# Splitting weight blocks behind the evacuation, and attention halves six items ahead

## The chip, the cores and the metric

The kernel runs on one core of one Trainium2 chip. The metric is the device time of one execution in microseconds (us); the median of several runs is compared. TensorE (PE) multiplies matrices; its loads of stationary operands are shown apart as PEld. VectorE (DVE) and ScalarE (ACT) evacuate results and prepare operands, GpSimd (POOL) starts accumulating DMAs and does a few small operations, and SyncE (SP) starts most DMAs.

## The reference

One decoder layer over 512 tokens of width 1024, in float32. A combined input projection gives q, k and v for three attention branches and three gate vectors; the branch outputs are projected, gated, summed and projected once more; two layer norms, a squared-ReLU MLP and a gated per-layer embedding follow.

```python
proj = x @ w_in
(da_q, da_k, da_v, sb_q, sb_k, sb_v, dl_q, dl_k, dl_v, gates) = jnp.split(proj, _split_points(), axis=-1)
o_da = diff_attention(...)            # 4 heads, two softmax maps per head
o_sb = stick_breaking_attention(...)  # 8 heads
o_dl = dilated_attention(...)         # 3 groups x 4 heads
g = jax.nn.sigmoid(gates).reshape(B, S, N_BRANCHES, D)
merged = (g[:, :, 0] * (o_da @ w_branch_da) + g[:, :, 1] * (o_sb @ w_branch_sb)
          + g[:, :, 2] * (o_dl @ w_branch_dil))
m = merged @ w_out
x = layer_norm(DEEPNORM_ALPHA * x + m, ln1_g, ln1_b)
c = jnp.square(jax.nn.relu(x @ w_up)) @ w_down
ple = jax.nn.sigmoid(x @ w_ple_gate) * (p @ w_ple)
x = layer_norm(DEEPNORM_ALPHA * x + c + ple, ln2_g, ln2_b)
```

## The kernel before

**Halves.** Each float32 operand of a large product is split into a high half in the rounded matmul type (fp32r) and a low half, the remainder. A product of two such operands takes three matmuls: high by high, high by low, low by high. A weight block is 128 x 1024 numbers. It is loaded by SP into one of five `raw` buffers (`RAW = 5`, line 223, function `fill`), cast by ACT into `wh` (line 255), and DVE subtracts to make `wl` (line 258); both lie in rings of seven (`RING = 7`). `split_next` does this for the next block in a fixed list (`chunks`). Some blocks are sums of two loaded ones; DVE adds them in place first (line 244). Other sums are made in DRAM by accumulating DMAs on POOL (line 190), after copies that SP starts (line 186).

**Items.** The work of PE is a list of 312 items, each with the blocks it needs, the blocks it releases (`it["c"]`), a function `mm` that issues its matmuls into a PSUM bank, and a function `ev` that evacuates the bank. Items 0 to 58 are the input projections: a T item makes 128 columns of q or k (24 products of 0.39 us each, one block), and a group of four V items makes 512 columns of v with four blocks, released by the last. Items 59 to 72, 73 to 86 and 95 to 108 are the three gates, each done with seven instead of eight block products (`seven`), two items for each product `p`, r = 0 and 1, with two blocks. Items 87 to 94, 109 to 116 and 117 to 124 are the three branch projections (`branch`, twelve products per item); they need the halves `oTh`, `oTl` of the attention outputs, which `halves(k)` makes on ACT or DVE (cast, lines 93 and 95) and DVE (line 574). Items 125 to 132 are the output projection, 133 to 154 the embedding gate and the embedding itself, 155 to 302 the MLP as alternating groups of up items (line 881 on) and down items (line 968 on), and from 303 the last block row, done plainly. In three up and three down groups of the MLP ("mixed") and in the second and third gate some of the blocks are sums made by DVE. Attention itself runs beside the items: generators for the heads are advanced by `step()`, between items and in the middle of a T item.

**The loop.** For item n the program runs the functions hooked to n (`at`, among them `halves` and the sigmoids), splits blocks that the item can't do without, issues the evacuation of item n-1, calls `pump`, starts other work that is due by number (the load of `pT` at item `first_branch + 3` = 112), issues the matmuls of n, adds the blocks that it releases to `freed`, and calls `pump` again. `pump(limit, most)` splits up to `most` blocks while fewer than `freed + 7` are split, and lets `fill` issue the loads that the raw buffers allow. From item 10 on both calls have `most` = 2.

**Order.** Each engine takes its own instructions strictly in the order of its queue. That order is made when the kernel is built: a planner in the framework goes through the program with its own estimates of durations, takes what it holds to be ready, and settles ties by the order in which the program wrote the instructions. It also gives out the 46 slots of 128 x 512 numbers in SBUF (`slot`) in which q, k, v, evacuated results, attention outputs and halves lie. So an edit of the program's order moves priorities, not places.

## Time and profile before

| what | value |
|---|---|
| median of 3 runs | 1076.69 us (1075.1 to 1078.05) |
| the profiled execution | 1074.75 us |
| its span, first to last instruction | 1073.1 us |
| PE busy | 1047.6 us, 98% |
| PEld busy | 898.1 us, 84% |
| DVE busy | 775.9 us, 72% |
| ACT busy | 557.2 us, 52% |
| POOL busy | 87.2 us, 8% |
| granted TensorE clock, mean | 0.994 |
| DMA | 209.12 MB, mean 195 GB/s |

The profile is of one execution, taken by the hardware profiler. A row of the timeline gives start, duration, engine, line of the program, operation, output and inputs, and in brackets how long the engine had been idle and what released it. Matmuls overlap: a product is shown with 0.39 us and one starts every 0.23 us. In the groups, "x245" is the count, followed by the busy time, the mean duration in ns, and the idle time just before with its releaser. The granted clock (PEclk) is the share of full speed that the chip allowed TensorE. The chain is the work that ended last, followed back from the end through what released each step.

### The profile page before, as it was taken

What the parts mean: (1) busy time and instruction counts of PE and PEld (TensorE: products, weight loads), DVE (VectorE), ACT (ScalarE), POOL (GpSimd) and SP (SyncE); (2) the same over time, 40 slices, a digit from 0 to 9 for tenths busy, and PEclk for the clock granted to TensorE, in tenths of its full rate; (3) what the DMA queues carried; (4) which work ended last, traced back from release to release, by engine and by line L of the source; (5) the groups of instructions that cost most, each with busy time, mean ns of one, the idle gap of its engine ahead of it and who ended that gap; (6) DMA issues with size and microseconds to landing.
All of it is one profiled execution on the core that took longest, in us unless ns stands there. A gap on an engine that the chain in (4) does not pass through costs nothing.

```text
span 1073.1 us, 14737 instructions
## 1 busy us (share of the span) xinstructions
PE 1047.6 (98%) x5503; PEld 898.1 (84%) x5503; DVE 775.9 (72%) x1328; ACT 557.2 (52%) x908; POOL 87.2 (8%) x107
## 2 busy tenths in 40 slices
PE   9999999999999899999999899999999999999996
PEld 6877788999888688888888788888989989989985
DVE  6888576545453567987757765898788788788786
ACT  6566444435242445786626322365756556557551
POOL 0000101000010100101101100100001011110000
PEclk9999999999999999999999999999999999999999
DMA  7454564428888664375967975347867978976712
GB/s 273 158 216 177 197 255 100 97 75 238 236 256 208 172 207 138 94 240 138 298 176 228 323 250 163 116 151 247 250 201 204 287 185 215 275 181 196 234 59 79
DMA packets 64140, 209.12 MB, mean 195 GB/s; under 512 B 7501, under 2 KB 10461, under 8 KB 62916
## 3 DMA queue, kind: packets, MB, share of 16 engines
q1 hardware_dynamic: 43108, 167.38, 43.2%
q0 software_dynamic: 20384, 39.88, 21.5%
q8 instruction: 43, 0.70, 0.2%
q10 hardware_dynamic: 576, 0.92, 0.2%
q14 instruction: 29, 0.24, 0.1%
HBM read 206.03 MB, written 77.62 MB: 264 GB/s over the span
## 4 chain that ended last, share of the span: by engine, by line
PE 95%; DVE 3%; ACT 1%; issue 1%; DMA 0%; POOL 0%; DVEq 0%; SPq 0%; ACTq 0%
PE mm L84 6%; PE mm L85 6%; PE mm L86 6%; PE mm L881 5%; PE mm L882 5%; PE mm L883 5%; PE mm L363 3%; PE mm L365 3%; PE mm L364 3%; PE at L451 3%; PE at L453 3%; PE at L454 3%; PE mm L968 2%; PE mm L969 2%; PE mm L970 2%; PE mm L600 2%
## 5 line engine op out<-in xcount | busy, mean ns | idle before, releaser
L255 ACT CAST wh<-raw 128x1024 fp32r<-128x1024 f32 x245 | 254.9, 1049 | 250.9 <-PE mm L85 44.6
L258 DVE TENSOR_TENSOR wl<-raw,wh 128x1024 fp32r<-128x1024 f32 x245 | 296.5, 1223 | 112.5 <-ACT wh L255 103.9
L84 PE MATMUL mm<-xhT,wh 128*128 128x512 f32 x304 | 121.6, 400 | 1.3 <-DVE da_qb L105 1.1
L86 PE MATMUL mm<-xhT,wl 128*128 128x512 f32 x304 | 119.6, 394 | 0.0
L85 PE MATMUL mm<-xlT,wh 128*128 128x512 f32 x304 | 119.6, 393 | 0.0
L881 PE MATMUL mm<-XH,wh 128*128 128x256 f32 x256 | 72.8, 285 | 5.1 <-DVE xn L975 2.5
L882 PE MATMUL mm<-XL,wh 128*128 128x256 f32 x256 | 72.5, 283 | 0.0
L883 PE MATMUL mm<-XH,wl 128*128 128x256 f32 x256 | 72.5, 283 | 0.0
L84 PEld LDWEIGHTS mm<-xhT,wh 128*128 128x128 f32 x304 | 57.5, 189 | 15.1 <-issue 3.9
L86 PEld LDWEIGHTS mm<-xhT,wl 128*128 128x128 f32 x304 | 57.4, 189 | 12.4 <-DVE wl L258 0.4
L85 PEld LDWEIGHTS mm<-xlT,wh 128*128 128x128 f32 x304 | 57.5, 189 | 10.8
L363 PE MATMUL mm<-wh,xhT 128*128 128x512 f32 x160 | 64.1, 402 | 0.0
L365 PE MATMUL mm<-wh,xlT 128*128 128x512 f32 x160 | 63.3, 396 | 0.0
L364 PE MATMUL mm<-wl,xhT 128*128 128x512 f32 x160 | 63.2, 395 | 0.0
L881 PEld LDWEIGHTS mm<-XH,wh 128*128 128x128 f32 x256 | 49.1, 192 | 6.5 <-issue 4.6
L882 PE MATMUL mm<-xs,wh 128*128 128x256 f32 x192 | 54.4, 283 | 0.0
L883 PE MATMUL mm<-xs,wl 128*128 128x256 f32 x192 | 54.4, 283 | 0.0
L881 PE MATMUL mm<-xs,wh 128*128 128x256 f32 x192 | 54.4, 283 | 0.0
L882 PEld LDWEIGHTS mm<-XL,wh 128*128 128x128 f32 x256 | 49.1, 192 | 0.2
L883 PEld LDWEIGHTS mm<-XH,wl 128*128 128x128 f32 x256 | 49.1, 192 | 0.0
L190 POOL DMA_DIRECT2D total<-total x26 | 23.9, 936 | 279.9 <-ACT wh L255 264.5
L365 PEld LDWEIGHTS mm<-wh,xlT 128*128 128x128 f32 x160 | 38.0, 238 | 3.8
(421 smaller groups left out, 2563.2 us busy)
## 6 DMA issues: line engine op xcount, KB each, us to landing
raw<-total SPq DMA_DIRECT2D x72, 512.0 KB, 5.8
raw<-in_wt_dram SPq DMA_DIRECT2D x38, 512.0 KB, 7.0
total<-in_wu_dram SPq DMA_DIRECT2D x26, 512.0 KB, 8.4
total<-total POOLq DMA_DIRECT2D x26, 512.0 KB, 9.3
raw<-in_wd_dram SPq DMA_DIRECT2D x25, 512.0 KB, 5.5
raw<-in_wu_dram SPq DMA_DIRECT2D x24, 512.0 KB, 4.9
total<-in_wd_dram SPq DMA_DIRECT2D x22, 512.0 KB, 7.3
raw<-in_wv_dram SPq DMA_DIRECT2D x20, 512.0 KB, 4.0
```

The source lines that it names most:

```text
L84: nc.tensor.matmul(ps, wh, xh, start=start, stop=False, skip_group_check=True)
L85: nc.tensor.matmul(ps, wh, xl, start=False, stop=False, skip_group_check=True)
L86: nc.tensor.matmul(ps, wl, xh, start=False, stop=stop, skip_group_check=True)
L255: i = nc.vector.tensor_copy(h, raw) if c.get("dve") else nc.scalar.copy(h, raw)
L258: i = nc.vector.tensor_sub(lo, raw, h.bitcast(F32))
L363: nc.tensor.matmul(ps, x1, c["h"][:, s], start=k == 0, stop=False)
L364: nc.tensor.matmul(ps, x1, c["l"][:, s], start=False, stop=False)
L365: nc.tensor.matmul(ps, x2, c["h"][:, s], start=False, stop=k == 7)
L451: nc.tensor.matmul(ps, h, c["h"][:, s], start=k == 0 and begins, stop=False, skip_group_check=True)
L881: nc.tensor.matmul(o, c["h"][:, s], h, start=first, stop=False, skip_group_check=True)
L882: nc.tensor.matmul(o, c["h"][:, s], lo, start=False, stop=False, skip_group_check=True)
L883: nc.tensor.matmul(o, c["l"][:, s], h, start=False, stop=last, skip_group_check=True)
```

## The change

Four edits. In `branch`, `halves(k)` is hooked to item `b0 - 6 + k` and not `b0 - 4 + k`, `b0` being the branch's first item. In the mixed groups of the MLP, block 3 is split ahead of block 4, and block 3 is released by the item that uses it last, not together with blocks 4 and 7. The `pump` behind the evacuation splits one block, and two only where `st["split"] - freed`, the blocks split and not yet released, is at most 3. The `pump` behind an item's matmuls splits nothing from item 10 on (it did not before item 10 either) and only lets `fill` issue loads.

```diff
@@ -575,7 +575,7 @@
                 oTs[4 * i + k] = (h, lo)
 
             for k in range(4):
-                hook(b0 - 4 + k, lambda k=k: halves(k))
+                hook(b0 - 6 + k, lambda k=k: halves(k))
 
@@ -838,8 +838,8 @@
             def mixed_chunks(w, first):
                 raw = {q: load(w[q], 1024) for q in (*first, 5, 3, 7)}
                 c = {p: chunk_of(raw[{6: 5, 4: 5}.get(p, p)], {6: raw[3], 4: raw[2]}.get(p))
-                     for p in (*first, 5, 6, 4, 3, 7)}
-                return c, {6: [], 5: [c[5], c[6]], 7: [], 3: [], 4: [c[4], c[3], c[7]]}
+                     for p in (*first, 5, 6, 3, 4, 7)}
+                return c, {6: [], 5: [c[5], c[6]], 7: [], 3: [c[3]], 4: [c[4], c[7]]}
 
@@ -1616,7 +1616,7 @@
             if prev is not None:
                 prev[0]["ev"](prev[1])
 
-            pump(freed, {1: 3, 3: 0, 4: 0}.get(n, 1 if n < 10 else 2))
+            pump(freed, {1: 3, 3: 0, 4: 0}.get(n, 1 if n < 10 or st["split"] - freed > 3 else 2))
@@ -1657,7 +1657,7 @@
             for _ in it["mm"](ps) or ():
                 step()
             freed += len(it["c"])
-            pump(freed, 0 if n < 10 else 2)
+            pump(freed, 0)
             prev = (it, ps)
         prev[0]["ev"](prev[1])
```

## The prediction

> **What bounds the kernel now.** I read the page's head and its chain first, then the waits of PE, then the windows in which PE is not busy throughout, and last the order of time around each stop.

> ```profile
> span 1073.1 us, 14737 instructions
> ...
> PE 1047.6 (98%) x5503; PEld 898.1 (84%) x5503; DVE 775.9 (72%) x1328; ACT 557.2 (52%) x908; POOL 87.2 (8%) x107
> ...
> PE 95%; DVE 3%; ACT 1%; issue 1%; DMA 0%; POOL 0%; DVEq 0%; SPq 0%; ACTq 0%
> ...
> L255 ACT CAST wh<-raw 128x1024 fp32r<-128x1024 f32 x245 | 254.9, 1049 | 250.9 <-PE mm L85 44.6
> L258 DVE TENSOR_TENSOR wl<-raw,wh 128x1024 fp32r<-128x1024 f32 x245 | 296.5, 1223 | 112.5 <-ACT wh L255 103.9
> ```

> TensorE is the bound: 95% of the chain that ended last. The change adds and removes no instruction; it only moves the splits (cast L255, 1.05 us, subtraction L258, 1.22 us) and the halves. So it can win only PE's idle time, 1073.1 - 1047.6 = 25.5 us, and what the clock loses behind a stop.

> ```profile
> 0.00:25.00 25.00, 22.80 (x89) 16.31 (x90) 16.35 (x30) 16.86 (x24) 1.70 (x10) 1.00 0.81 275
> ...
> 1050.00:1075.00 25.00, 14.66 (x77) 12.43 (x75) 14.54 (x35) 3.26 (x8) 2.06 (x3) 0.85 0.22 82
> ```

> Of the 25.5 us, 25.00 - 22.80 = 2.2 lie in the start, whose rules (items below 10) stay, and 23.1 - 14.66 = 8.4 in the last 23.1 us, where all blocks are split. That leaves 14.9 us in the middle, and the waits of PE name nearly all of it (time, count, longest):

> ```profile
> PE at L1466 <- DVE dl_k L322: 2.8, 1, 2.8
> PE mm L881 <- DVE xn L975: 2.5, 3, 0.8
> PE mm L598 <- ACT oTh L93: 1.7, 1, 1.7
> PE mm L600 <- DVE oTl L574: 1.6, 1, 1.6
> PE mm L881 <- DVE cut L893: 1.4, 1, 1.4
> PE at L1130 <- DVE rel L1166: 1.3, 1, 1.3
> PE mm L881 <- ACT wh L255: 1.1, 1, 1.1
> PE mm L84 <- DVE da_qb L105: 1.1, 1, 1.1
> PE at L1531 <- DVE L L1515: 1.0, 1, 1.0
> PE at L1355 <- DVE ah L1345: 0.9, 1, 0.9
> ```

> Only one of these is a wait for a split itself (wh, 1.1 us). The others are waits for evacuations (dl_k, xn, cut) and halves (oTh, oTl) that stood in the queue of DVE or ACT behind something. That is the kind of wait that this change moves.

> **Where the splits go.** I counted block numbers through the 312 items by both rules, with no times. Call the lead the blocks split and not yet released. Before, it is 7 ahead of almost every item. A T item releases one block: the old rule splits its replacement at once, ahead of its evacuation. By the new rule the evacuation comes first, then one split if the lead is above 3. After a V block of four items has released 4 blocks the lead is 3, gets 2, and from then on each T item finds 5 and leaves 4. So the lead settles at 4 to 5 in the projections and the first two gates, 5 to 7 later, and no item from 10 on finds its blocks missing except items 129 and 303, where one block is split ahead as before. With a lead of 5 the ring place of the next block has been free for two items, so its cast need not start when an item ends, which is when the evacuation is wanted.

> **Stop 1, at 357 us.** (Start, duration, engine, line; in brackets the idle time before and who ended it.)

> ```profile
> 354.44 1.04 ACT L255 CAST wh<-raw 128x1024 fp32r<-128x1024 f32 x1 [6.87 <-PE mm L85]
> 355.51 1.23 DVE L258 TENSOR_TENSOR wl<-raw,wh 128x1024 fp32r<-128x1024 f32 x1 [6.69 <-ACT wh L255]
> ...
> 356.66 0.68 DVE L322 COPY dl_k<-mm 128x512 f32<-128x512 f32 x1
> ...
> 357.40 1.78 PE L1466 MATMUL at<-dl_k,dl_q 128*128 128x128 f32 x8 [2.81 <-DVE dl_k L322]
> ```

> The item ended at 357.40 - 2.81 = 354.6. DVE, free for 6.69 us, waited for the cast, subtracted, and only then evacuated dl_k, 0.74 us after whose start PE went on. With the evacuation first PE goes on at 354.65 + 0.74 = 355.4: gain 2.0 us. What follows (L1515 and da_qb, 2.1 us) hangs on the head's own chain of DVE and ACT, which starts at L1466 and keeps its length: it shifts, and I give it no gain.

> **Stop 2, at 615 us.**

> ```profile
> 600.49 1.05 SPq L1263 DMA_DIRECT2D pT<-in_pT_dram  x2
> ...
> 611.94 1.05 ACT L255 CAST wh<-raw 128x1024 fp32r<-128x1024 f32 x1 [8.46 <-PE mm L600]
> ...
> 614.29 1.14 ACT L93 CAST oTh<-oT 128x512 fp32r<-128x512 f32 x2
> ...
> 616.51 0.69 DVE L574 TENSOR_TENSOR oTl<-oT,oTh 128x512 fp32r<-128x512 f32 x1
> ```

> The program writes the last branch's halves at items 113 to 116, yet all four come behind the casts that item 116 released, though ACT had been idle for 8.46 us. The load of pT, written at item 112 and first in line for slots, is what they stand behind, I take it; the trace doesn't name the reason. Two items earlier, two of the four are written ahead of it, and no post-item split stands before the other two. PE's two stops were 1.70 + 1.55 = 3.25 us. The third half is used six products into the item (6 x 0.23 = 1.4 us), the fourth nine: behind the two evacuation steps of item 116, each about as long as the 0.68 us of L322, I still expect 0.8 us of waiting.

> The stop also cost clock. Chain in order of time (start, duration), and two windows (PE, PEld, DVE, ACT, POOL busy, then PEclk):

> ```profile
> 618.04 0.43 PE mm L598
> ...
> 620.88 0.23 PE mm L599
> ```

> ```profile
> 350.00:375.00 25.00, 20.15 (x99) 15.83 (x98) 15.41 (x58) 10.81 (x27) 3.68 (x4) 0.93 0.61 154
> 600.00:625.00 25.00, 21.75 (x88) 17.27 (x87) 17.73 (x26) 5.26 (x6) 2.69 (x3) 0.93 1.06 321
> 700.00:725.00 25.00, 24.96 (x114) 20.07 (x112) 24.61 (x38) 16.10 (x27) 0.93 (x2) 1.00 0.47 153
> ...
> 750.00:775.00 25.00, 23.55 (x197) 23.38 (x196) 18.05 (x22) 17.40 (x26) 1.76 (x2) 1.00 0.80 245
> ```

> From 618.0 to 620.6 six products stepped by 0.43 us and not 0.23: 6 x 0.20 = 1.2 us. The granted clock is 0.93 in just these two windows; around the stop of 1.4 us (750 to 775) it is 1.00. So stop 2 gives 3.25 + 1.2 - 0.8 = 3.6 us. (At stop 1 the clock's share is lost again: the head's chain, not PE, sets the pace there.)

> [...] The trace shows the slow step behind stops of 2.81 and 3.25 us, so the rows decide. [...]

> **Stops 3, in the MLP.**

> ```profile
> 802.66 2.95 ACT L255 CAST wh<-raw 128x1024 fp32r<-128x1024 f32 x3 [2.66 <-DVE raw L244]
> ...
> 803.75 3.50 DVE L258 TENSOR_TENSOR wl<-raw,wh 128x1024 fp32r<-128x1024 f32 x3 [0.58 <-ACT wh L255]
> ...
> 807.16 0.68 DVE L975 TENSOR_TENSOR xn<-xn,mm 128x512 f32<-128x512 f32 x1
> ```

> ```profile
> 751.35 1.22 DVE L258 TENSOR_TENSOR wl<-raw,wh 128x1024 fp32r<-128x1024 f32 x1
> 752.48 0.69 DVE L893 TENSOR_TENSOR cut<-cut,mm 128x512 f32<-128x512 f32 x1
> ```

> Three times (L975) the end of a mixed down group releases three blocks at once and DVE makes three subtractions before the evacuation that frees PE's bank. By the new frees block 3 goes earlier and the splits come one per item behind the evacuation: the burst is gone, and 2.5 us with it. At 752 the evacuation stands behind one subtraction; ahead of it, it gains 1.1 of the 1.4 us. Swapping blocks 3 and 4 of a mixed group moves one addition (L244) by one place; the block is first used eight or more items later, so it is hidden. The wh stop (1.1 us) I leave at nothing: its block is split two items later, and that can go either way.

> Gains: 2.0 + 3.6 + 2.5 + 1.1 = 9.2 us.

> **What it can cost.** The halves of the other two branches go two items up; among PE's waits above there is none of a gate's products, and the halves free their sources earlier: nothing. SP issues its loads behind the splits, so loads come later by as many blocks as splits do; the sums on POOL hang on the third last cast and shift with it. The price of that shift is nowhere in the trace. Its low end is 0, the lead being at least 4 everywhere. Two places are tight. Around 700 to 725 DVE is busy 24.61 of 25 us, and three blocks that were split before go into it: 3 x 1.22 = 3.7 us at most. In the second gate the count puts block 96 one item ahead of its first use, where it was three:

> ```profile
> 501.17 1.22 DVE L244 TENSOR_TENSOR raw<-raw,raw 128x1024 f32<-128x1024 f32 x1
> ...
> 511.01 2.36 DVE L258 TENSOR_TENSOR wl<-raw,wh 128x1024 fp32r<-128x1024 f32 x2 [0.26 <-ACT wh L255]
> ```

> ```profile
> L598 PE MATMUL mm<-wh,oTh x96: 389/389/628, 531.5 to 642.3; 128*128 128x512 f32 x96
> ```

> Item 87 starts at 531.5. Items are 12 x 0.23 = 2.7 us, so item 81 starts at 531.5 - 6 x 2.7 = 515.3 and wants block 96 half way, at 516.6. Its subtraction, the first of the pair at 511.01, ended at 512.2: 4.4 us in hand. Block 91, whose place in the raw ring the chain of loads and additions up to block 96 waits for, moves back by up to three items, 8.1 us; then PE would wait 3.7 us, and the clock would cost 1.2: 4.9. Its ring place and data are there as before, so I expect only part of the delay. Over both places that is 0 to 8.6 us; I take 2.5, nearer to zero, as the lead is 4 at its lowest and both engines have slack outside these windows.

> **Sum.** 1074.75 (the profiled execution: span 1073.1 and 1.65 around it) - 9.2 + 2.5 = 1068.05. The median of the runs shown, 1076.69, lies 1.94 above the profiled execution, so 1070.0 is predicted.

> **Rivals.** (a) Most stops go elsewhere. The planner orders each engine by its own estimate of readiness, with the program's order as priority; it may put a split, whose place is now free early, ahead of the evacuation after all, or hold the halves as before. Then only the burst and stop 1 gain, 4.5, against 2.5 lost: 1076.69 - 2.0 = 1074.7, no change. For it: at 614 the order was not the program's. Against: at 354 and 803 it was, and these gains need only that. That the change does nothing at all (1076.7) is its extreme.

> (b) Slower: the lead of 4 runs out. The second and third gate have the same list of blocks, so twice 4.9, and 3.7 in the window at 700: 13.5 lost, 1076.69 - 9.2 + 13.5 = 1081.0. It decides from 9.2 + 3.2 = 12.4 us on. For it: DVE's 24.61 of 25. Against: PE waited only 1.1 us for splits in the whole middle, and the ring places come free no later than before. [...]

> (c) Better: the wh stop and the 2.1 us behind stop 1 vanish too and nothing is lost: 1076.69 - 9.2 - 3.2 = 1064.3.

> **How the numbers follow.** The forecast gets 0.52, (c) 0.08, (a) 0.26, (b) 0.14. A measurement of this kernel tells about 0.3%, 3.2 us, from no change. The forecast's own range is 1066 to 1073.4, and so faster has 0.60, the same 0.26, slower 0.14. The range runs from (c), 1063.5 with the scatter of the runs, to 1079, which takes in (a) and leaves out most of (b).

> **What would show it.** Right: no wait of L1466 on dl_k above 1 us; granted clock 1.00 in both windows; no three L258 in a row ahead of L975 near 807, 886 and 966; two of the oTh casts before 612. Wrong: waits of PE on wh or wl between 500 and 530 or 690 and 730, or new waits on evacuations elsewhere.

## The result and the profile after

The changed kernel takes 1068.36 us (median of 4 runs, 1066.74 to 1069.17), the one before 1075.89 in the same comparison: ratio 0.9925, 95% interval 0.9905 to 0.9946, so 8.1 us faster. The prediction was 1070.0. The time came out close. Where it came from did not, in one of the three places that were to gain, and the loss stands elsewhere than was named.

The page of the changed kernel, head and chain; its profiled execution took 1068.38 us, the span is 1066.7 of it:

```profile
span 1066.7 us, 14724 instructions
...
PE 1044.9 (98%) x5503; PEld 896.6 (84%) x5503; DVE 773.1 (72%) x1328; ACT 557.6 (52%) x908; POOL 86.1 (8%) x107
...
PE 91%; DVE 4%; ACT 3%; DMA 1%; issue 1%; POOL 0%; DVEq 0%; SPq 0%
```

TensorE is still the bound. Of the span's 6.4 us, 25.5 - 21.8 = 3.7 are idle time of PE and 1047.6 - 1044.9 = 2.7 are products that ran faster: one slow step of the clock less (behind a stop, two before and one after, each 3.41 us at a granted 0.50) is half of 3.41 us, 1.7; what makes the rest is not settled. The waits of PE after (total, times, longest):

```profile
PE at L1466 <- DVE dl_k L322: 2.8, 1, 2.8
PE at L135 <- ACT da_ka L126: 2.6, 1, 2.6
PE at L344 <- ACT wh L255: 1.6, 1, 1.6
PE at L1130 <- DVE rel L1166: 1.3, 1, 1.3
PE at L1399 <- DVE lg L1394: 1.1, 1, 1.1
PE at L451 <- ACT XH L733: 1.0, 1, 1.0
PE at L1491 <- DVE r L1484: 1.0, 1, 1.0
```

The waits on oTh, oTl, xn, cut and on the MLP's wh are gone, and so are those on da_qb and L. dl_k is as it was, and da_ka, lg, XH and r are new. (These names are tiles of the program: dl_k, da_ka and da_v hold k or v of an attention branch, lg and r stand in a softmax, XH is a high half.) Windows of the changed kernel (length, busy time of PE, PEld, DVE, ACT, POOL, then PEclk):

```profile
350.00:375.00 25.00, 20.77 (x105) 16.12 (x103) 12.59 (x54) 8.40 (x23) 1.78 (x2) 1.00 0.69 199
375.00:400.00 25.00, 22.52 (x108) 19.15 (x109) 18.84 (x50) 12.82 (x30) 0.00 (x0) 0.93 0.50 163
...
600.00:625.00 25.00, 25.00 (x110) 20.21 (x109) 18.77 (x27) 4.63 (x5) 2.67 (x3) 1.00 0.97 272
...
700.00:725.00 25.00, 23.98 (x107) 19.27 (x106) 23.57 (x37) 15.16 (x27) 0.00 (x0) 1.00 0.56 189
...
750.00:775.00 25.00, 25.00 (x211) 25.00 (x210) 18.84 (x22) 19.25 (x29) 1.76 (x2) 1.00 0.90 272
```

Put side by side by the start of the same product in both traces, the changed kernel is behind by 0.8 us at 28 us, 1.2 at 345, 3.2 at 400, 4.1 at 520; then ahead by 1.0 at 666, 3.0 at 766, 4.1 at 834, 5.0 at 898, 6.2 at 980 and 6.4 at the end. So stop 2 gave 4.1 + 1.0, some 5.0 us, what follows to the end of the MLP 2.0 + 3.1 = 5.1, and 4.1 were lost before 520 us, some 3 of them after 345.

### The profile page after: what moved, and what is told of

Read it like the earlier page. It is cut to its first block, busy times and chain, and to the rows that moved or that the text cites. A ratio compares the mean times of both kernels' runs of the same rounds, so it can differ in the third digit from the quotient of the medians.

```text
span 1066.7 us, 14724 instructions
## 1 busy us (share of the span) xinstructions
PE 1044.9 (98%) x5503; PEld 896.6 (84%) x5503; DVE 773.1 (72%) x1328; ACT 557.6 (52%) x908; POOL 86.1 (8%) x107
## 3 DMA queue, kind: packets, MB, share of 16 engines
q0 software_dynamic: 20384, 39.88, 21.8%
## 4 chain that ended last, share of the span: by engine, by line
PE 91%; DVE 4%; ACT 3%; DMA 1%; issue 1%; POOL 0%; DVEq 0%; SPq 0%
PE mm L84 6%; PE mm L85 6%; PE mm L86 6%; PE mm L883 5%; PE mm L882 5%; PE mm L881 5%; PE mm L363 3%; PE mm L364 3%; PE mm L365 3%; PE at L451 3%; PE at L454 3%; PE at L453 3%; PE mm L968 2%; PE mm L970 2%; PE mm L969 2%; PE mm L598 2%
## 5 line engine op out<-in xcount | busy, mean ns | idle before, releaser
L258 DVE TENSOR_TENSOR wl<-raw,wh 128x1024 fp32r<-128x1024 f32 x245 | 296.6, 1221 | 118.1 <-ACT wh L255 115.9
L255 ACT CAST wh<-raw 128x1024 fp32r<-128x1024 f32 x245 | 255.0, 1050 | 233.6 <-PE mm L600 33.2
L84 PE MATMUL mm<-xhT,wh 128*128 128x512 f32 x304 | 121.0, 398 | 0.4 <-DVE sb_v L376 0.3
L86 PE MATMUL mm<-xhT,wl 128*128 128x512 f32 x304 | 119.3, 392 | 0.1
L85 PE MATMUL mm<-xlT,wh 128*128 128x512 f32 x304 | 119.3, 392 | 0.0
L881 PE MATMUL mm<-XH,wh 128*128 128x256 f32 x256 | 72.4, 283 | 0.0
L84 PEld LDWEIGHTS mm<-xhT,wh 128*128 128x128 f32 x304 | 57.2, 188 | 14.5 <-issue 2.7
L86 PEld LDWEIGHTS mm<-xhT,wl 128*128 128x128 f32 x304 | 57.1, 188 | 12.4 <-DVE wl L258 0.5
L85 PEld LDWEIGHTS mm<-xlT,wh 128*128 128x128 f32 x304 | 57.2, 188 | 10.9
L881 PE MATMUL mm<-xs,wh 128*128 128x256 f32 x192 | 54.3, 283 | 0.0
L881 PEld LDWEIGHTS mm<-XH,wh 128*128 128x128 f32 x256 | 49.1, 192 | 0.3
```

The lines of the kernel that those rows point to most:

```text
L84: nc.tensor.matmul(ps, wh, xh, start=start, stop=False, skip_group_check=True)
L85: nc.tensor.matmul(ps, wh, xl, start=False, stop=False, skip_group_check=True)
L86: nc.tensor.matmul(ps, wl, xh, start=False, stop=stop, skip_group_check=True)
L255: i = nc.vector.tensor_copy(h, raw) if c.get("dve") else nc.scalar.copy(h, raw)
L258: i = nc.vector.tensor_sub(lo, raw, h.bitcast(F32))
L881: nc.tensor.matmul(o, c["h"][:, s], h, start=first, stop=False, skip_group_check=True)
```

## The experiments

All ratios are against the kernel before, with the 95% interval.

| kernel | median us | ratio |
|---|---|---|
| the change | 1068.36 | 0.9925 (0.9905 to 0.9946) |
| halves_only | 1071.94 | 0.9961 (0.9947 to 0.9976) |
| splits_only | 1070.75 | 0.9949 (0.9937 to 0.9961) |
| mixed_only | 1074.14 | 0.9976 (0.9967 to 0.9986) |
| halves_mixed | 1068.98 | 0.9933 (0.9919 to 0.9946) |
| full_lead | 1067.37 | 0.9917 (0.9903 to 0.9931) |
| pT_late | 1070.07 | 0.9938 (0.9925 to 0.9952) |
| tied | 1060.91 | 0.9856 (0.9843 to 0.9870) |
| tied_dve | 1071.04 | 0.9942 (0.9927 to 0.9957) |
| tied_all | 1065.54 | 0.9902 (0.9887 to 0.9918) |
| tied_full | 1059.35 | 0.9850 (0.9837 to 0.9863) |

**One part of the change at a time**, on the kernel before.

```
# halves_only
-                hook(b0 - 4 + k, lambda k=k: halves(k))
+                hook(b0 - 6 + k, lambda k=k: halves(k))
# splits_only
-            pump(freed, {1: 3, 3: 0, 4: 0}.get(n, 1 if n < 10 else 2))
+            pump(freed, {1: 3, 3: 0, 4: 0}.get(n, 1 if n < 10 or st["split"] - freed > 3 else 2))
-            pump(freed, 0 if n < 10 else 2)
+            pump(freed, 0)
# mixed_only
-                     for p in (*first, 5, 6, 4, 3, 7)}
-                return c, {6: [], 5: [c[5], c[6]], 7: [], 3: [], 4: [c[4], c[3], c[7]]}
+                     for p in (*first, 5, 6, 3, 4, 7)}
+                return c, {6: [], 5: [c[5], c[6]], 7: [], 3: [c[3]], 4: [c[4], c[7]]}
```

> The kernel before with one edit: halves at b0 - 6 + k. Theory 1 (of the prediction): the halves of the last branch were late because the load of pT stood ahead of them; two items earlier they come ahead of it, the stops on oTh and oTl (1.7 + 1.6 us) and the slow clock behind them (1.2 us) go, all other stops stay: 1075.9 - 4.5 = 1071.4. Rival: they were late because of the two splits that item 116 adds ahead of its evacuation; this edit leaves those, the stops stay, 1075.9.

> The kernel before with both edits of the split rule (none behind an item's products, one behind an evacuation where more than three blocks are ahead), halves and mixed groups as before. Theory 1: the stop on oTh and oTl stays; the new waits of the projections are there (da_ka 2.6 us with a slow step, lg 1.1); the stops on cut (1.4) and wh (1.1) go, those on xn partly: between 1073 and 1077. Rival: the splits of item 116 were what held the halves; then this edit alone frees them, 1069 to 1072, nearly the whole result.

> The kernel before with one edit: block 3 of a mixed group is split and released ahead of block 4. Theory 1: the three stops on xn (0.8 us each) come from three blocks that are released at once; now two are, the burst is two subtractions long and the stops shrink or go: gain 0 to 2.5 us, 1073.4 to 1075.9, and nothing else moves. Rival: the burst comes from the two splits allowed behind an item's products and in front of its evacuation; then the stops stay at 2.5 us and the time at 1075.9.

Each part alone gains: 4.2, 5.5 and 2.6 us (1 minus the ratio, times 1076.6). That is 12.3 together, and the change gained 8.1: the parts cure the same stops. By the profiles, the stops on xn go in splits_only and in mixed_only, 3.1 us in each; stop 2 gives 3.5 in halves_only, 2.8 in splits_only and 5.0 in the change. That counts 3.1 + 1.3 = 4.4 twice, about the 4.2 that are missing.

halves_only came out as its theory said, 1071.94 against 1071.4, and mixed_only at 1074.14 within 1073.4 to 1075.9. splits_only did not: 1070.75 is below its theory's 1073 to 1077 and within its rival's 1069 to 1072. The waits of PE in splits_only:

```profile
PE at L1466 <- DVE dl_k L322: 2.8, 1, 2.8
PE at L135 <- ACT da_ka L126: 2.6, 1, 2.6
...
PE mm L600 <- DVE oTl L574: 0.6, 1, 0.6
PE mm L598 <- DVE cut L604: 0.5, 1, 0.5
PE mm L598 <- ACT oTh L93: 0.3, 1, 0.3
```

It has the new da_ka wait and no wait on xn, and of stop 2 only 1.4 us is left. VectorE there, in the kernel before and then in splits_only, whose products are 4.3 us later at this point:

```profile
613.03 1.23 DVE L258 TENSOR_TENSOR wl<-raw,wh 128x1024 fp32r<-128x1024 f32 x1 [1.03 <-ACT wh L255]
614.77 1.22 DVE L258 TENSOR_TENSOR wl<-raw,wh 128x1024 fp32r<-128x1024 f32 x1
```

```profile
617.33 1.22 DVE L258 TENSOR_TENSOR wl<-raw,wh 128x1024 fp32r<-128x1024 f32 x1 [1.03 <-DMA raw<-in_wo_dram]
618.47 0.68 DVE L574 TENSOR_TENSOR oTl<-oT,oTh 128x512 fp32r<-128x512 f32 x1
```

All four halves are still late, ScalarE's casts at 617.19 and 618.66, but one subtraction and not two stands ahead of the first oTl: it starts at 618.47 - 4.3 = 614.2 by the time of the kernel before, where it was 616.51. So its rival was right in part: the splits of item 116 lengthened the stop, though they are not what kept the halves from running earlier.

So the split rule makes the loss in the projections and gains at stop 2 and in the MLP, where the two other edits gain too. In mixed_only stop 2 stands and xn no longer appears; the earlier split and release of block 3 alone remove all three stops of 0.83 us:

```profile
PE at L1466 <- DVE dl_k L322: 2.8, 1, 2.8
PE mm L598 <- ACT oTh L93: 1.7, 1, 1.7
PE mm L600 <- DVE oTl L574: 1.6, 1, 1.6
PE mm L881 <- DVE cut L893: 1.4, 1, 1.4
```

**The change without its split rule** (the halves and the mixed groups only):

> The changed kernel with the split rule of before (the first and third edits alone, no edit of where splits go). Theory S: the split rule is worth little beside the other two, as what it takes away at 615, 752 and in the MLP overlaps with them and it loses at 374 and 462: the other two alone give the sum of their own gains, 1076.6 - 4.7 - 2.5 = 1069.4, within 1.5 us of the changed kernel. Rival: the rule carries the result: 1072 or more.

1068.98 us, 0.9933 against 0.9925. The intervals overlap almost wholly: with the other two edits in place, the rule that names the change adds nothing that these runs can tell.

**The lower lead.**

```
# full_lead, on the changed kernel
-            pump(freed, {1: 3, 3: 0, 4: 0}.get(n, 1 if n < 10 or st["split"] - freed > 3 else 2))
+            pump(freed, {1: 3, 3: 0, 4: 0}.get(n, 1 if n < 10 else 2))
```

> The changed kernel without the threshold: always up to two splits behind an evacuation, none behind an item's products. Theory L (of the prediction): the lower lead costs up to some us; with the full lead 1068.4 - 2.5 = 1066, the waits on da_ka, lg, and XH shrink. Rival H: the planner fills the ring as soon as a place is free, whatever item a split is written at, so the threshold hardly matters: 1067.4 to 1069.4 with the same waits. Rival: pairs of splits in front of evacuations come back in the MLP, 1070 or more.

1067.37 us, at the edge of rival H's range and not told apart from the change (0.9903 to 0.9931 against 0.9905 to 0.9946); theory L's 1066 is just outside the interval. Not all waits are as in the change, though: dl_k (2.8) and da_ka (2.5) stay, lg and XH are gone, da_v (0.8) and oTh (0.4) have come. Whether one or two blocks are split behind an evacuation moves small waits about; its worth, 1.0 us by the medians, is less than these runs can tell.

**What the halves stood behind.**

```
# pT_late, on the kernel before
-            if n == first_branch + 3:
+            if n == first_branch + 8:
                 load_pT()
```

> The kernel before with one edit: the load of pT is written five items later (item 117, behind the four halves of the last branch), the halves stay at b0 - 4. Theory pT (of the prediction): the halves stand behind pT in line for slots; now all four run before 612, the stops on oTh and oTl (1.7 + 1.6) and the slow clock (1.2 to 1.4) go: 1076.6 - 4.5 = 1072. Rival: something else holds the halves (the casts of item 116, or slots that come free only then); the stops stay and the time is 1076.6.

1070.07 us, 6.6 faster than before (5.2 to 8.1 by the interval) with not one split or half moved in the program; between 573 and 667 us its profile gains 5.4. The casts of oTh on ACT, order of time, in pT_late and then in the changed kernel:

```profile
589.83 0.61 ACT L93 CAST oTh<-oT 128x512 fp32r<-128x512 f32 x1
594.68 0.61 ACT L93 CAST oTh<-oT 128x512 fp32r<-128x512 f32 x1
```

```profile
591.58 0.62 ACT L93 CAST oTh<-oT 128x512 fp32r<-128x512 f32 x1
616.94 0.62 ACT L93 CAST oTh<-oT 128x512 fp32r<-128x512 f32 x1
```

Before, both stood at 614.29. With pT behind the halves all four run before 600 (the two on VectorE at 594.03 and 596.90), and no wait on oTh or oTl is left. In the changed kernel one of ACT's two, and one of VectorE's (594.05), come early and the others wait until 616 to 619. That is two of the four ahead of pT, as predicted. What pT_late shows is that the load of pT keeps the halves back; that it does so by taking slots first stays an assumption.

**Where the evacuations stand.** In the tied kernels each split is queued, on the engines named, behind the evacuation that the program puts ahead of it (order only, no wait):

```
# tied, on the changed kernel; tied_dve: VectorE alone; tied_all: from item 35 to the end
             if prev is not None:
+                traced = nc.cur_bb.bb.instructions
+                mark = traced[-1]
                 prev[0]["ev"](prev[1])
+                if 35 <= n < 60:
+                    k = next(k for k in reversed(range(len(traced))) if traced[k] is mark)
+                    tie[:] = list({i.engine: i for i in traced[k + 1:] if i.engine in TIED}.values())
+                elif n == 60:
+                    tie.clear()
...
+        TIED = (mybir.EngineType.DVE, mybir.EngineType.Activation)
```

> The changed kernel, where in items 35 to 59 each split is queued on ScalarE and VectorE behind the evacuation that the program puts ahead of it. Theory A: the waits on dl_k (2.8 us) and da_ka (2.6 us, and 1.7 us of slow clock) are there because the planner pulls a split, whose ring place is free, ahead of the evacuation again; held back, both shrink to under 1 us, the granted clock is 1.00 throughout the middle, and the time is 1068.4 - 2.0 - 3.6 = 1062 to 1065. Rival B: the evacuations are late for another reason (the end of the head's own chain, or the load), the waits stay and the time is 1068.4 or more, as PE then waits on wh or wl.

> As the tied kernel (1060.9), but only VectorE's subtraction is queued behind the evacuation, not ScalarE's cast. Theory: the wait on dl_k is VectorE's order (subtraction ahead of dl_k) and goes; the wait on da_ka is ScalarE's order (a cast whose load has not landed, ahead of da_ka) and stays with its slow clock: about 1064.5, half way. Rival: one of the two orders decides both: 1061 or 1068.

> As the tied kernel (1060.9), but from item 35 to the end. Theory: outside the projections no evacuation waits behind a split for long (waits left: XH 1.1, lg 0.9, da_qb 1.3), so at most 1 to 2 us more: 1059 to 1061. Rival: splits held back in the gates and in the MLP come late where VectorE is nearly full (700 to 725 us): waits on wh and wl, 1063 or more.

Tied: 1060.91 us, 7.5 better than the change, and more than theory A gave (1062 to 1065). Between 345 and 400 us it gains 7.7 us on the changed kernel. The waits on dl_k, da_ka and r (2.8 + 2.6 + 1.0) and the slow step (1.7) are gone there, and one on da_qb (1.3) has come: 6.8 of the 7.7. In the changed kernel (rows of three engines, in order of time):

```profile
347.49 0.39 PE L86 MATMUL mm<-xhT,wl 128*128 128x512 f32 x1
347.72 1.68 PE L1450 MATMUL at<-dl_k,dl_q 128*128 128x128 f32 x8
...
348.81 1.23 DVE L258 TENSOR_TENSOR wl<-raw,wh 128x1024 fp32r<-128x1024 f32 x1 [3.54 <-ACT wh L255]
...
355.60 1.04 ACT L255 CAST wh<-raw 128x1024 fp32r<-128x1024 f32 x1 [6.83 <-PE mm L85]
356.68 1.23 DVE L258 TENSOR_TENSOR wl<-raw,wh 128x1024 fp32r<-128x1024 f32 x1 [6.64 <-ACT wh L255]
357.82 0.68 DVE L322 COPY dl_k<-mm 128x512 f32<-128x512 f32 x1
...
374.51 1.04 ACT L255 CAST wh<-raw 128x1024 fp32r<-128x1024 f32 x1 [2.77 <-DMA raw<-in_wga_dram]
375.46 0.59 ACT L122 ACTIVATE da_ka<-mm 64x512 fp32r<-64x512 f32 x1
...
377.23 0.39 PE L135 MATMUL at<-da_ka,da_qa 128*128 128x256 f32 x1 [2.57 <-ACT da_ka L126]
```

And in the tied kernel:

```profile
347.86 1.68 PE L1450 MATMUL at<-dl_k,dl_q 128*128 128x128 f32 x8
348.06 0.69 DVE L322 COPY dl_k<-mm 128x512 f32<-128x512 f32 x1 [2.65 <-PE mm L86]
...
369.07 0.59 ACT L122 ACTIVATE da_ka<-mm 64x512 fp32r<-64x512 f32 x1
...
371.45 1.05 ACT L255 CAST wh<-raw 128x1024 fp32r<-128x1024 f32 x1
```

In the tied kernel dl_k's evacuation is released by PE's L86, the last product ahead of L1450 at 347.86. So its item is, in the changed kernel too, the one that ends ahead of L1450, at 347.7 there, a whole item before the stop. Its evacuation was ready then, and stood 10 us in VectorE's queue behind two subtractions, the second of which had to wait for a cast that could not start: that cast waits for PE's L85, which frees its ring place (6.83 us). The cast at 374.51 waits 2.77 us for its load with da_ka's evacuation behind it. Both splits are written in the program behind these evacuations, and the planner queued them ahead; on what estimate it did so, no trace shows. Held back, dl_k is copied 0.2 us after its item ends.

tied_dve tells the two orders apart. dl_k's wait is gone, da_ka's is there:

```profile
PE at L135 <- ACT da_ka L126: 2.6, 1, 2.6
PE at L1413 <- ACT da_v L93: 1.4, 1, 1.4
```

So the first is VectorE's order and the second ScalarE's, as expected. The time is not: 1071.0 and not 1064.5, no better than the change (0.9942 against 0.9925, intervals overlapping). By the profiles VectorE's order does gain, 4.3 us on the changed kernel between 345 and 365 us, but 7.1 are lost again by 420: the clock has three slow steps (0.50 for 3.41 us each, from 373.41, 376.82 and 404.13 us) where the changed kernel has one (from 377.98), and casts still stand ahead of da_ka (at 371.12, after 2.58 us of waiting for PE's L85) and da_v. tied_all is slower than tied (0.9902 against 0.9856). Its rival gave the sign, not the wait: PE waits 2.0 us on cut for L794, near 696 us, an evacuation and not wh or wl; another 2.6 us are lost in the last 60 us, where PE has no wait, for a reason that I have not settled.

> The tied kernel (1060.9) with two more edits: from item 60 on always up to two splits behind an evacuation, and the load of pT five items later. Theory: XH (1.1 us), which was there only where the threshold was, goes, the halves all run before 612, and nothing else moves: 1059 to 1060.5. Rival: pairs of splits ahead of evacuations make new waits, as on da_v (0.8) in the full-lead kernel: 1061 or more.

```
# tied_full, on the tied kernel
-            pump(freed, {1: 3, 3: 0, 4: 0}.get(n, 1 if n < 10 or st["split"] - freed > 3 else 2))
+            pump(freed, {1: 3, 3: 0, 4: 0}.get(n, 1 if n < 10 or n < 60 and st["split"] - freed > 3 else 2))
-            if n == first_branch + 3:
+            if n == first_branch + 8:
                 load_pT()
```

1059.35 us, ratio 0.9850: the best median here, as expected, though its interval overlaps that of tied. The waits on XH (1.1) and, nearly, lg are gone, and the longest that PE has left is 1.3 us.

## Why the prediction was right, and where it was not

**Stop 1: predicted 2.0 us, came to nothing.** The step that failed is "The item ended at 357.40 - 2.81 = 354.6 ... With the evacuation first PE goes on at 354.65 + 0.74 = 355.4". It holds two errors. dl_k was not waiting for the item that ended there: its own item had ended a whole item earlier, at 346.5 in the kernel before (row below) and at 347.7 in the changed one, and since then its evacuation stood in a queue.

```profile
346.51 1.68 PE L1450 MATMUL at<-dl_k,dl_q 128*128 128x128 f32 x8
```

And the evacuation did not come first: rival (a) named this, "it may put a split ... ahead of the evacuation after all". The reason given against it, that the ring place "has been free for two items", fails on 355.60 [6.83 <-PE mm L85]: the cast queued ahead of dl_k had no place yet, so the lead counted by the program's order is not the lead on the chip. The gain was there, and larger than thought; it needed the queue held, which tied does. The bracket on the clock at this stop is borne out: halves_only has the wait on dl_k without a slow step behind it (1.00 from 356.79 to 360.20 us), and gains only 0.3 us between 345 and 400 us.

**Stop 2: predicted 3.6, measured 5.0.** That pT was the reason was an assumption; pT_late now shows it. Idle 3.25 and the clock were right in kind. The clock was sized too low: 1.2 us was six slow products, and 5.0 - 3.25 = 1.75 is about half of a whole step of 3.41 us (0.50 from 617.16 to 620.57 us in the kernel before). The 0.8 us of remaining wait did not come. What the prediction did not price by itself is the two splits ahead of the halves: splits_only, in which the halves are still late, takes 2.8 of the 5.0 us away, so part of the gain comes from either edit.

**Stops 3: predicted 2.5 + 1.1, measured 5.1, with a new wait of 1.0 (XH) taken off.** xn went wholly, and to either edit: mixed_only and splits_only both lack it. With what PE lost behind them the three stops were worth 3.1. cut gave all of its 1.4, and the wh stop (1.1), left at nothing, went too; both stay in halves_mixed, which lacks only the split rule, so they are the rule's. By the profiles the rule wins 3.3 us on halves_mixed after 520 us and loses 2.0 between 345 and 520, which is why the times hardly tell the two kernels apart. VectorE in the changed kernel, where three subtractions stood before:

```profile
797.18 2.36 DVE L258 TENSOR_TENSOR wl<-raw,wh 128x1024 fp32r<-128x1024 f32 x2
799.46 0.68 DVE L975 TENSOR_TENSOR xn<-xn,mm 128x512 f32<-128x512 f32 x1
```

The picture of "splits come one per item behind the evacuation" is wrong here too: two still stand ahead of it, and two are short enough.

**The cost: predicted 2.5, measured about 4, elsewhere.** There is no wait on wh or wl at 516 or 700 to 725, the two places named, and by full_lead the lower lead costs nothing that is clear of the scatter (1.0 us by the medians). The loss is 2.0 us between 345 and 400 (da_ka 2.6 and r 1.0 came, da_qb and L, 2.1, went; the slow step moved from 357 to 378), 1.1 at 457 (lg), and 0.8 at the start. The last is not the change's, as far as the runs show: the wait of L344 on wh is between 0.3 and 1.9 us over the twelve profiles, though no edit touches the items below 10.

Of the marks named, four were met (three subtractions ahead of L975 gone, two oTh casts early, clock 1.00 in both windows, no wait on wh or wl in the two tight places; the first of the two windows by luck, as its slow step only moved into the next) and two were not: L1466 still waits 2.8 us, and there are new waits on evacuations.

So the sum, 9.2 - 2.5 = 6.7 against 6.4 in the profiled executions, was right by luck in the number: a gain that failed (2.0) and a cost that was larger (by about 1.5) stood against two gains that were larger (by 1.4 and 1.5). The mechanism held at stop 2 and in the MLP, and not at stop 1 and in the cost.

## What to carry to other kernels

Where a planner orders the queues, moving an instruction later in the program only lowers its priority; it can be queued ahead all the same, and what is ready behind it is then held up: here dl_k's evacuation, ready at 347.7 us, was copied at 357.82, though VectorE was idle for 6.64 us in between, ahead of the split that was queued first. Look for the row whose idle time ends at another engine, with a ready evacuation behind it, and bind the order of those two where it matters (in 25 items: 7.5 us; to the end of the kernel: less). When several edits aim at stops, test each alone: here the parts' gains summed to 12.3 us and the whole gave 8.1.

## What the runs showed of the hardware

```profile
354.33:357.75 3.42, 0.61 (x5) 0.35 (x4) 2.23 (x5) 1.04 (x1) 0.87 (x1) 1.00 0.19 13
357.75:361.16 3.41, 3.41 (x14) 2.93 (x13) 3.19 (x25) 1.97 (x8) 0.00 (x0) 0.50 0.98 206
```

```profile
354.08:357.50 3.42, 1.71 (x8) 1.09 (x6) 0.82 (x1) 1.04 (x1) 0.00 (x0) 1.00 1.18 372
357.50:360.91 3.41, 2.35 (x14) 2.13 (x15) 3.41 (x22) 0.84 (x4) 0.00 (x0) 1.00 0.78 257
374.56:377.98 3.42, 0.60 (x3) 0.30 (x3) 2.36 (x3) 3.35 (x6) 0.00 (x0) 1.00 1.05 284
377.98:381.39 3.41, 3.41 (x12) 3.05 (x13) 2.37 (x9) 1.14 (x4) 0.00 (x0) 0.50 0.95 357
```

```profile
353.37:356.79 3.42, 1.47 (x7) 0.89 (x5) 1.01 (x1) 1.04 (x1) 0.75 (x1) 1.00 0.02 6
356.79:360.20 3.41, 2.54 (x15) 2.13 (x15) 3.41 (x22) 1.03 (x5) 0.12 (x1) 1.00 0.79 115
```

Between 10 and 1050 us the traces of the kernel before and of the changed one have three such windows with less than 1.7 us of PE: 0.61 and 0.73 before (the second from 613.75 us) and 0.60 after. Each is followed by a whole window at 0.50; the one with 1.71 us in the changed kernel is not, nor is the one with 1.47 in halves_only. In tied_dve windows with 1.28 and 1.44 us (from 369.99 and 400.71 us) are followed by one at 0.50. Busy time is not the whole of it: the second of the two slow windows in a row follows one in which PE was busy for 2.92 us. The 2.8 us on dl_k lie in one window in the kernel before (3.42 - 0.61) and across two in the changed kernel (1.71 + 1.06) and in halves_only (1.95 + 0.87). So a stop of 2.6 to 2.8 us cost up to 1.7 us of clock (half of 3.41) or nothing here, by how these windows cut it.
